# Two octets' stores cut into 112 partitions and 5, 5, 5 and 1, in a linear attention kernel that waits for its DMA engines

## The chip, the cores and the metric

The kernel runs on one core of one Trainium2 chip. The metric is the device time of an execution in microseconds; medians of several executions are quoted. "Span" is the time from the first to the last instruction in a profile; it is about 1.9 us less than the device time.

## The reference

```python
# Q, K, V: [8, 12, 512, 64] float32
Q_feat = np.maximum(0, Q)
K_feat = np.maximum(0, K)
KV = np.einsum('bhkd,bhkv->bhdv', K_feat, V)
K_sum = np.sum(K_feat, axis=2)
numerator = np.einsum('bhqd,bhdv->bhqv', Q_feat, KV)
denominator = np.einsum('bhqd,bhd->bhq', Q_feat, K_sum)
return numerator / (denominator[:, :, :, None] + 1e-10)
```

## The kernel before

The 96 heads are worked on in twelve groups of eight, the octets (`NO` = 12). K, V and Q come in through GpSimd DMAs that cast to bf16. An octet's output, 1 MB of float32 in 128 partitions of 8 KB, is stored by one DMA that SyncE issues and the core's 16 DMA engines carry out; the last octet's store is cut in two along the row. A copy of 128 bytes into `scratch` holds each of the first stores back until the loads five octets ahead have landed.

```python
def store(o, o_sb):
    if o + DELAY < NO:
        nc.sync.dma_start(out=scratch, in_=k_sb[2 * (o + DELAY)][0:1, 0, :])
    parts = 2 if o == NO - 1 else 1
    n = RQ // parts
    for j in range(parts):
        rs = slice(n * j, n * (j + 1))
        nc.sync.dma_start(out=Or[o].rearrange("p (r d) -> p r d", d=D)[:, rs], in_=o_sb[:, rs])
# ... (all else is untouched)
```

## Time and profile before

| | before |
|---|---|
| device time | 127.98 us (median of 3, 127.97 to 128.13) |
| span of the profile | 126.2 us |
| last compute instruction ends | 120.0 us |
| last completion mark of the last store | 125.28 us |
| last instruction | 126.19 us |

How to read it: between 120.0 and 125.28 us nothing but stores runs. The lines of the profile that show the DMA engines' load stand in the prediction below.

Two kinds of records are used besides the profile's views. A *completion mark* is the count of one that each DMA engine adds to a transfer's semaphore (the counter that a waiting engine watches) behind its share of the transfer. It is a packet of 4 bytes. A *packet* is one run of bytes that an engine moves, with its duration. Neither names its engine.

### The profile page before, as it was taken

How to read it: one execution, taken by the hardware profiler on the slowest of the kernel's cores; microseconds unless marked ns; L12 is line 12 of the kernel's file. 1: busy time of each engine (PE TensorE's matmuls, PEld its weight loads, DVE VectorE, ACT ScalarE, POOL GpSimd, SP SyncE). 2: the span in 40 equal slices, each digit the busy share in tenths (PEclk: the TensorE clock that was granted, in tenths of full speed). 3: DMA queues.
4: the chain of work that ended last, by engine and by line, in shares of the span. 5: the costliest groups of instructions: out<-in, count | busy, mean ns of one | idle time of the engine just before them, and what ended most of it. 6: DMA issues, size and time to landing. Idle time of an engine off the chain costs nothing.

```text
span 126.2 us, 4865 instructions
## 1 busy us (share of the span) xinstructions
PE 77.3 (61%) x2112; PEld 68.3 (54%) x2112; DVE 80.6 (64%) x210; ACT 76.9 (61%) x169; POOL 32.1 (25%) x62
## 2 busy tenths in 40 slices
PE   0032917978397956534997647389964793797200
PEld 0041907967386845434986646178953692696100
DVE  3256785698936959673669787528828628774900
ACT  0165891599198798660799949508917925958000
POOL 6902424325243331241143133033113000000000
PEclk9999999999859999996799999955999679769995
DMA  3999999999999999999999999999999999999992
GB/s 106 374 309 213 214 208 209 217 206 218 205 215 209 208 214 324 257 216 325 256 215 301 280 214 281 301 212 214 347 235 216 316 266 216 352 418 410 416 384 104
DMA packets 10757, 32.81 MB, mean 260 GB/s; under 512 B 1392, under 2 KB 1392, under 8 KB 9328
## 3 DMA queue, kind: packets, MB, share of 16 engines
q0 software_dynamic: 8064, 17.83, 73.9%
q1 hardware_dynamic: 2384, 13.63, 27.1%
q10 hardware_dynamic: 288, 1.05, 2.1%
q8 instruction: 16, 0.26, 0.7%
q14 instruction: 5, 0.04, 0.1%
HBM read 37.75 MB, written 12.58 MB: 399 GB/s over the span
## 4 chain that ended last, share of the span: by engine, by line
DMA 32%; PE 27%; issue 13%; ACT 11%; DVE 10%; ACTq 1%; SPq 0%
DMA v_sb<-in_V_dram 25%; PE ps_out L174 13%; PE ps_kv L139 11%; DMA kv_first<-in_K_dram 7%; ACT kvd L146 5%; ACT qt L159 4%; PE ps_qt L153 3%; DVE o_sb L187 3%; DVE qt L121 3%; ACT vo L134 3%; DVE kf L128 2%; DVE vo L130 1%; DVE rec L186 1%; ACTq L267 0%; DVE kvd L118 0%
## 5 line engine op out<-in xcount | busy, mean ns | idle before, releaser
L139 PE MATMUL ps_kv<-vo,kf 128*128 128x130 bf16 x384 | 32.5, 248 | 21.9 <-ACT vo L134 11.7
L174 PE MATMUL ps_out<-kvd,qt 128*32 128x130 bf16 x1536 | 33.7, 243 | 16.7 <-issue 13.3
L139 PEld LDWEIGHTS <-kf 128*128 128x128 bf16 x384 | 27.8, 112 | 25.3 <-DVE vo L130 16.3
L174 PEld LDWEIGHTS <-qt 128*32 128x32 bf16 x1536 | 27.0, 107 | 21.9 <-issue 15.3
L146 ACT CAST kvd<-ps_kv 64x130 bf16<-64x130 f32 x96 | 25.2, 263 | 16.7 <-PE ps_kv L139 14.8
L134 ACT ACTIVATE vo<-v_sb,mask 128x1024 bf16<-128x1024 bf16 x22 | 26.2, 1190 | 13.9 <-DMA v_sb<-in_V_dram 13.8
L187 DVE TENSOR_TENSOR o_sb<-ps_out,rec 128x768 f32<-128x768 f32 (+1 forms) x36 | 31.3, 868 | 1.4
L159 ACT ACTIVATE qt<-ps_qt 128x512 bf16<-128x512 bf16 x48 | 24.8, 603 | 0.3
L128 DVE TENSOR_SCALAR kf<-k_sb,mask 128x1024 bf16<-128x1024 bf16 x44 | 19.1, 476 | 8.6 <-DMA k_sb<-in_K_dram 8.6
L85 POOL DMA_DIRECT2D k_sb<-in_K_dram x22 | 12.8, 583 | 39.1 <-DMA q_sb<-in_Q_dram 24.1
L184 DVE TENSOR_SCALAR den<-ps_out 128x12 f32<-128x12 f32 (+1 forms) x36 | 5.9, 164 | 17.9 <-PE ps_out L174 17.8
L153 PE MATMUL ps_qt<-ident,q_sb 128*128 128x128 bf16 x192 | 15.7, 245 | 2.4 <-issue 2.4
L87 POOL DMA_DIRECT2D v_sb<-in_V_dram x22 | 12.3, 557 | 17.1 <-DMA k_sb<-in_K_dram 7.3
L153 PEld LDWEIGHTS <-q_sb 128*128 128x128 bf16 x192 | 14.0, 112 | 2.6 <-issue 2.5
L130 DVE TENSOR_SCALAR vo<-v_sb,mask 128x1024 bf16<-128x1024 bf16 x22 | 10.6, 481 | 2.1 <-DMA v_sb<-in_V_dram 2.1
L186 DVE RECIPROCAL rec<-den 128x12 f32<-128x12 f32 (+1 forms) x36 | 7.9, 220 | 1.2
L91 POOL DMA_DIRECT2D q_sb<-in_Q_dram x12 | 6.5, 542 | 7.8 <-DMA v_sb<-in_V_dram 4.1
L128 DVE TENSOR_SCALAR kf<-kv_first,mask 128x1024 bf16<-128x1024 f32 x4 | 2.8, 750 | 4.9 <-DMA kv_first<-in_K_dram 4.9
L134 ACT ACT_TABLE_LOAD x1 | 1.3, 1283 | 5.8 <-DMA kv_first<-in_V_dram 5.8
L121 DVE MEMSET qt<- 128x2048 f32 x2 | 3.5, 1765 | 0.8 <-issue 0.8
L134 ACT ACTIVATE vo<-kv_first,mask 128x1024 bf16<-128x1024 f32 x2 | 2.4, 1180 | 2.6 <-DMA kv_first<-in_V_dram 2.6
L130 DVE TENSOR_SCALAR vo<-kv_first,mask 128x1024 bf16<-128x1024 f32 x2 | 1.5, 747 | 0.0
(12 smaller groups left out, 3.5 us busy)
## 6 DMA issues: line engine op xcount, KB each, us to landing
out_dram<-o_sb SPq DMA_DIRECT2D x11, 1024.0 KB, 9.2
q_sb<-in_Q_dram POOLq DMA_DIRECT2D x12, 512.0 KB, 14.9
k_sb<-in_K_dram POOLq DMA_DIRECT2D x22, 256.0 KB, 13.8
v_sb<-in_V_dram POOLq DMA_DIRECT2D x22, 256.0 KB, 13.2
kv_first<-in_V_dram ACTq DMA_DIRECT2D x2, 512.0 KB, 7.3
kv_first<-in_K_dram SPq DMA_DIRECT2D x2, 512.0 KB, 7.0
out_dram<-o_sb SPq DMA_DIRECT2D x2, 512.0 KB, 5.1
scratch<-k_sb SPq DMA_DIRECT2D x7, 0.1 KB, 5.1
```

The lines of the kernel that those rows point to most:

```text
L85: nc.gpsimd.dma_start(out=k_sb[g].rearrange("p r d -> p (r d)"), in_=Kr[g])
L87: nc.gpsimd.dma_start(out=v_sb[g].rearrange("p r d -> p (r d)"), in_=Vr[g])
L128: nc.vector.tensor_scalar(kf[g][:, :, s, :], k_sb[g], scalar1=0.0, scalar2=mask[:, 0, s:s + 1], op0=Alu.max, op1=Alu.mult)
L130: nc.vector.tensor_scalar(vo[g % NB][:, :, 0, 0:D], v_sb[g], scalar1=mask[:, 1, 0:1], scalar2=None, op0=Alu.mult)
L134: nc.scalar.activation(vo[g % NB][:, :, 1, 0:D], v_sb[g], Act.Copy, scale=mask[:, 1, 1:2])
L139: nc.tensor.matmul(ps_kv[g], kf[g][:, r, :, :].rearrange("p s d -> p (s d)"), vo[g % NB][:, r, :, :], start=(r == 0), stop=(r == R - 1), s ...
L146: nc.scalar.copy(kvd[g % NK][64 * c:64 * c + 64, :, s, c, :], ps_kv[g][64 * s:64 * s + 64])
L153: nc.tensor.transpose(ps_qt[o, i][:, u, :], q_sb[o][:, i * (U // 2) + u, :], ident)
L159: nc.scalar.activation(qtz[o % NZ][:, z, us, :, z, :], pv[:, :, :, z, :], Act.Relu)
L174: nc.tensor.matmul(po[hs, b, c:c + 2 * D1], qtf[o % NZ][:, z, u * P + 32 * w:u * P + 32 * w + 32], kvd[(2 * o + h // 4) % NK][:, h % 4 // ...
L186: nc.vector.reciprocal(rec, den)
L187: nc.vector.tensor_tensor(o_sb[:, 2 * u0:2 * (u0 + nu)].rearrange("p (b r) d -> p b r d", b=2), pv[:, :, :, 0:D], rec.unsqueeze(3).to_broa ...
```

## The change

The intent: some DMA engines work off their queues two microseconds before others. Two stores, those of octets 1 and 3, are cut so that engines 0 to 4 take packets from the other eleven: the piece of 112 partitions is meant to leave each engine one packet short of its eight, and the three pieces of 5 are meant for engines 0 to 4 alone. One partition, the *lone row*, is left over. The prediction says by which rule packets go to engines.

```diff
+    def cuts(o):
+        return ((16, P), (0, 5), (5, 10), (10, 15), (15, 16)) if o in (1, 3) else ((0, P),)
...
-        parts = 2 if o == NO - 1 else 1
...
+        Ov = Or[o].rearrange("p (r d) -> p r d", d=D)
+        if o == NO - 1:
+            for j in range(2):
+                rs = slice(RQ // 2 * j, RQ // 2 * (j + 1))
+                nc.sync.dma_start(out=Ov[:, rs], in_=o_sb[:, rs])
+            return
+        for p0, p1 in cuts(o):
+            nc.sync.dma_start(out=Ov[p0:p1], in_=o_sb[p0:p1])
```

More of the change, by code (lines that the diff above doesn't have):

```diff
@@ L197, in store @@
             nc.sync.dma_start(out=scratch, in_=k_sb[2 * (o + DELAY)][0:1, 0, :])
-        parts = 2 if o == NO - 1 else 1
-        n = RQ // parts
-        for j in range(parts):
-            rs = slice(n * j, n * (j + 1))
-            nc.sync.dma_start(out=Or[o].rearrange("p (r d) -> p r d", d=D)[:, rs], in_=o_sb[:, rs])
+        Ov = Or[o].rearrange("p (r d) -> p r d", d=D)
[6 more added lines that the diff above has]
+            nc.sync.dma_start(out=Ov[p0:p1], in_=o_sb[p0:p1])
     zero(0)
```

## The prediction

> **What bounds the kernel now.** I read the page's slices first, then the windows, then the waits and issues of SyncE, then the trace's completion marks of single transfers. Three whole lines of the page's slices and queues:
>
> ```profile
> DMA  3999999999999999999999999999999999999992
> ...
> q0 software_dynamic: 8064, 17.83, 73.9%
> q1 hardware_dynamic: 2384, 13.63, 27.1%
> ```
>
> The mean busy share of the 16 DMA engines is 90% or more in every slice but the first and the last. q0 carries the casting loads; q1 carries the eleven 1 MB stores, the two halves of the last one, and two of the first loads. No compute engine comes near that (the busiest, DVE, is at 64% of the span). The windows view, by stretch (columns: busy us of each engine with its instruction count, clock, DMA share, GB/s):
>
> ```profile
> 75.00:104.00 29.00, 21.04 (x549) 18.49 (x552) 17.09 (x41) 18.09 (x42) 5.66 (x11) 0.82 1.08 264
> 104.00:120.00 16.00, 9.80 (x336) 8.37 (x322) 12.02 (x30) 9.38 (x22) 0.00 (x0) 0.89 1.04 362
> 120.00:121.50 1.50, 0.00 (x0) 0.00 (x0) 0.02 (x1) 0.00 (x0) 0.00 (x0) 1.00 1.00 415
> 121.50:122.50 1.00, 0.00 (x0) 0.00 (x0) 0.00 (x0) 0.00 (x0) 0.00 (x0) 1.00 0.93 381
> 122.50:123.50 1.00, 0.00 (x0) 0.00 (x0) 0.00 (x0) 0.00 (x0) 0.00 (x0) 0.63 0.65 266
> 123.50:124.90 1.40, 0.00 (x0) 0.00 (x0) 0.00 (x0) 0.00 (x0) 0.00 (x0) 0.50 0.38 155
> ```
>
> The reader is to see that a share over 1.00 is possible (packets of one engine overlap a little), that all engines are full up to 121.5 us, and that they then drop out one after another: 0.93, 0.65, 0.38. Compute is over at 120.0. So the kernel ends when the latest DMA engine has worked off its queue, and the idle time of the others between 121.5 and 124.9 is 0.07 + 0.35 + 0.62 x 1.4 = 1.3 us per engine. A perfect balance could win about that and no more.
>
> Who is late can be told from the 16 completion marks that each transfer leaves in the trace, one for each DMA engine. For the last half store (issued at 120.05) they come, counted from the first at 122.76 us, at 0, 0.02, 0.04, 0.07, 0.17, 0.64, 0.77, 1.21, 1.80, 2.16, 2.19, 2.21, 2.23, 2.32, 2.34 and 2.51 us. Five engines are early, eight are over 2.1 us behind the first. The spread is not there at the start (0.6 us for loads landing near 20 us); it is 1.5 at 30 us, 2.7 at 85 us, and the engines keep it. Its growth goes with the 16 instruction fetches:
>
> ```profile
> q8 instruction: 16, 0.26, 0.7%
> ```
>
> Each is one packet of 16 KB that takes 0.88 to 0.97 us on one engine; after the eighth, at 68.1, eight marks of a load stand over a microsecond behind, and after the ninth one mark stands at 2.6 us, so the same eight engines seem to be hit twice. The marks do not name their engine. That the early five are engines 0 to 4 I take from the change's words; the trace as packed can't confirm it.
>
> **What the Trainium skill says.** (1) "Runtime: NRT & Kernel Launch", section Instruction fetch mechanics: instructions are refilled in blocks of 16 KiB by the sequencer's own DMA queue. The trace agrees: 16 packets of 16,384 B on a queue of their own. (2) "DMA: Bandwidth & Descriptors", section Why a DMA increments its semaphore by 16 and not by 1: a transfer issued from SP runs on the largest k up to 16 that divides the slowest dimension, and on the lowest-numbered k engines. So 112 partitions give 7 packets to each of 16 engines, 5 partitions one packet to each of engines 0 to 4. One partition may be split: the 128-byte copies into `scratch` left 112 packets of 8 B in the trace, which is 7 copies over 16 engines, so a lone row of 8 KB would become 16 packets of 512 B. (3) Same page, section The descriptor swizzle: in a 128-partition transfer each engine serves one SBUF port by itself. (4) "SBUF — State Buffer", section Door 1: The DMA port swizzle: partitions 0 to 3 (with 32 to 35) share a port, the next four the next, and one port gives about 27 GB/s. An 8,192 B store packet here takes 309 ns, 26.5 GB/s: one engine alone fills a port. No run here shows two engines on one port.
>
> **The change part by part.** It touches octets 1 and 3 only. Their stores are issued in the middle:
>
> ```profile
> 53.49 0.58 SPq L202 DMA_DIRECT2D out_dram<-o_sb  x1
> ...
> 73.54 0.53 SPq L202 DMA_DIRECT2D out_dram<-o_sb  x1
> ...
> 84.08 0.50 SPq L197 DMA_DIRECT2D scratch<-k_sb  x1
> ```
>
> *Issuing.* Four more DMAs per octet at 0.53 us are 2.1 us of SyncE, in a queue that next acts at 62.9 and at 84.1. Hidden. The eight added DMAs go once round the eight semaphores that these DMAs use in turn, so the stores at the end meet the same ones as before. Seven output buffers take turns, so octet 1's is written again only for octet 8, long after. No new wait.
>
> *Late engines (5 to 15).* Each loses one packet of 8 KB an octet. Packets took 309 to 322 ns, but the durations add up to 1.08 or 1.09 of the time in the middle stretches, so one is worth 0.32 / 1.09 = 0.29 us. The lone row gives back perhaps 0.03 us (estimate: 512 of 8,192 B are 0.02 us, and some for the packet and its mark, 9 ns). Net -0.26 us an octet, **-0.5 us** for two. Being full to the end, these engines end that much earlier: the last mark at 124.75 instead of 125.28.
>
> *Early engines (0 to 4).* By count, +3 - 1 = 2 packets, 0.6 us an octet, 1.2 us for two. They would end at 1.2 to 1.4 us of the scale above, where the late ones end at 2.0. There is room, so by count the sum is -0.5 us: 127.98 - 0.5 = 127.5 us.
>
> *Ports.* By the skill's port table the cost is not only the count. In (0, 5) four engines read partitions 0 to 3 through one port: up to 4 x 0.31 = 1.24 us instead of 0.31. (5, 10) and (10, 15) put two or three on one port: up to 0.93 us each. If the early five run in step, which marks only 0.17 us apart suggest, the three rounds cost up to 3.1 us instead of 0.93, less the 0.31 removed: +2.8 us an octet at worst, 5.6 for two, against 2.5 us of slack. Queue q0's packets between them pull the engines apart and let a port be shared by fewer; I estimate 1 to 2 us an octet. The 112 partitions also no longer start at a port's edge: with seven consecutive ones to an engine, two engines sometimes share a port, and a quarter more time for 7 packets (0.5 us) would eat the gain of the late ones.
>
> **The rivals.** (a) *Count alone*: -0.5 us, 127.5. For it: the engines are full throughout and the lag is carried to the end; the choice of just two octets and five engines fits the marks. Against: it takes the port for free. (b) *Ports cost something*: the late engines gain nothing or lose 0.2 us an octet, the early five use up their slack: 128.0 to 129.2. For it: 26.5 GB/s a packet is a port's rate. Against: reads of SBUF come only from stores, at most half of the packets even during a store, and the queues may overlap behind a stalled packet. (c) *Full contention*: engines 0 to 4 become the new tail, +3 us, 131; it needs all five in step in both octets. (d) *The fetches move*: the eight new DMAs and their waits shift instruction blocks onto other engines, or the early five are not 0 to 4. In the latter case engines with 2.5 us of lag get 1.2 us more: 129.2. SyncE ran only 53 instructions, so that no new block is due. (e) *Hidden anyway*: loads that land 0.5 us sooner change nothing if compute sets the end. Compute ended at 120.0 with over 4 us of stores still queued, so this is unlikely.
>
> **Range and chances.** I give (a) about half, (b) four tenths, (c) and (d) the rest. The middle of that lies at 127.7. Low end: the full 0.6 us of two packets and some luck, 127.2. High end: the upper part of (b), 129.0. Faster by over 2% would need 125.4 us, 2.5 us less, twice what perfect balance gives: 0.01. Slower by over 2% means over 130.5 us, (c) alone: 0.05. Within 2%: 0.94.
>
> **What would show it right or wrong.** Right: the last store's marks span about 1.9 us instead of 2.5, early five at 1.2 to 1.4; the DMA share in the last 3.4 us is higher, its fall later and steeper; the 8 KB packets still take 309 to 322 ns; the queue's 8 KB packets fall from 1,408 to 1,376, with 32 of 512 B if the lone row is split. Ports: some dozens of 8 KB packets with 600 to 1,250 ns, right after 55 and 75 us, and 112-partition packets over 350 ns. A new tail: five marks of the late stores come last. The prediction is wrong if the marks' spread stays at 2.5 us or grows, or if the gain exceeds 1.3 us, which would mean that more than the balance of the end was changed.

## The result, and the profile after

The changed kernel took **127.87 us** (median of 6, 127.73 to 128.08), the kernel before in the same rounds 128.02 us (median of 6, 127.97 to 128.18). The ratio is 0.9987, with a 95% interval of 0.9974 to 1.0. Ratios here are the mean time of one kernel's runs over that of the other's of the same rounds, so not quite the ratio of the medians. Executions over 1.5% slower than the fastest of the same kernel are left out of the means. The gain is about 0.15 us, a quarter to a third of what the count of packets promised; as the interval reaches 1.0, it is not clear of noise.

The page of the changed kernel, the same lines as in the prediction:

```profile
DMA  3999999999999999999999999999999999999992
...
q0 software_dynamic: 8064, 17.83, 74.0%
q1 hardware_dynamic: 2416, 13.63, 27.0%
...
q8 instruction: 16, 0.26, 0.7%
```

The load of the engines is what it was. q1 has 32 packets more, and the trace shows that these are completion marks alone: 384 of 4 bytes instead of 352, while the packets of 8 KB are still 1,408. So the lone row of each cut store was *not* split into pieces of 512 B; it is one packet of 8 KB more on one engine, and leaves one mark: 2 x (16 + 5 + 5 + 5 + 1 - 16) = 32.

SyncE's issues, from the timeline (start, us, instruction, count):

```profile
53.24 1.95 SPq L210 DMA_DIRECT2D out_dram<-o_sb  x5
62.38 0.50 SPq L202 DMA_DIRECT2D scratch<-k_sb  x1
...
73.14 1.87 SPq L210 DMA_DIRECT2D out_dram<-o_sb  x5
83.28 0.50 SPq L202 DMA_DIRECT2D scratch<-k_sb  x1
```

Five DMAs are issued in 1.95 and 1.87 us, and SyncE is next needed over 7 us later: hidden, as predicted. The windows view of the end, with the columns of the prediction (the last two are DMA share and GB/s):

```profile
120.00:121.50 1.50, 0.00 (x0) 0.00 (x0) 0.17 (x1) 0.00 (x0) 0.00 (x0) 0.84 0.98 410
121.50:122.50 1.00, 0.00 (x0) 0.00 (x0) 0.00 (x0) 0.00 (x0) 0.00 (x0) 0.50 1.01 414
122.50:123.50 1.00, 0.00 (x0) 0.00 (x0) 0.00 (x0) 0.00 (x0) 0.00 (x0) 0.50 0.84 344
123.50:124.90 1.40, 0.00 (x0) 0.00 (x0) 0.00 (x0) 0.00 (x0) 0.00 (x0) 0.50 0.22 91
```

Against 0.93, 0.65 and 0.38 of before the share holds longer and then falls more steeply: 1.01, 0.84, 0.22. The balance is better, and yet the end moved little. The 16 completion marks of the last half store show it (us from the span's start):

```
before  122.76 122.78 122.80 122.83 122.93 123.40 123.53 123.97 124.56 124.92 124.95 124.97 124.99 125.08 125.10 125.28
after   122.96 122.98 123.09 123.85 124.06 124.09 124.10 124.12 124.18 124.19 124.28 124.33 124.54 124.58 124.60 125.12
```

Fifteen engines are done by 124.60, 0.68 us before the old end. One is done at 125.12. It alone sets the end, 0.16 us earlier than before. These are single profiles, and the last mark varies: in three further runs that leave every engine its packets (4, 5 and 6 below) it came at 125.42, 125.54 and 125.22 us. So the one mark that stands apart is the finding, not the 0.16 us. Which engine it is, and why, is what the experiments had to find.

### The profile page after: what moved, and what is told of

It is laid out like the page before. It is cut to its first block, busy times and chain, and to the rows that moved or that the text cites. A ratio compares the mean times of both kernels' runs of the same rounds, so it can differ in the third digit from the quotient of the medians.

```text
span 126.0 us, 4878 instructions
## 1 busy us (share of the span) xinstructions
PE 77.5 (62%) x2112; PEld 68.7 (54%) x2112; DVE 80.8 (64%) x210; ACT 77.1 (61%) x169; POOL 31.2 (25%) x62
## 4 chain that ended last, share of the span: by engine, by line
DMA 35%; PE 27%; DVE 13%; issue 13%; ACT 6%; ACTq 1%; SPq 0%; DVEq 0%
DMA v_sb<-in_V_dram 28%; PE ps_out L174 13%; PE ps_kv L139 11%; DMA kv_first<-in_K_dram 7%; DVE o_sb L187 4%; DVE kf L128 3%; PE ps_qt L153 3%; DVE qt L121 3%; ACT kvd L146 3%; DVE vo L130 2%; ACT vo L134 2%; ACT qt L159 2%; DVE rec L186 1%; ACTq L275 1%; DVE den L184 0%
## 5 line engine op out<-in xcount | busy, mean ns | idle before, releaser
L174 PE MATMUL ps_out<-kvd,qt 128*32 128x130 bf16 x1536 | 35.2, 251 | 16.8 <-issue 13.8
L139 PE MATMUL ps_kv<-vo,kf 128*128 128x130 bf16 x384 | 31.5, 242 | 22.9 <-ACT vo L134 12.8
L139 PEld LDWEIGHTS <-kf 128*128 128x128 bf16 x384 | 26.8, 109 | 26.1 <-DVE vo L130 16.7
L174 PEld LDWEIGHTS <-qt 128*32 128x32 bf16 x1536 | 28.6, 111 | 22.0 <-issue 15.5
L85 POOL DMA_DIRECT2D k_sb<-in_K_dram x22 | 12.3, 561 | 39.2 <-DMA q_sb<-in_Q_dram 24.7
L153 PE MATMUL ps_qt<-ident,q_sb 128*128 128x128 bf16 x192 | 15.2, 241 | 1.3 <-issue 1.0
```

The lines of the kernel that those rows point to most:

```text
L85: nc.gpsimd.dma_start(out=k_sb[g].rearrange("p r d -> p (r d)"), in_=Kr[g])
L139: nc.tensor.matmul(ps_kv[g], kf[g][:, r, :, :].rearrange("p s d -> p (s d)"), vo[g % NB][:, r, :, :], start=(r == 0), stop=(r == R - 1), s ...
L153: nc.tensor.transpose(ps_qt[o, i][:, u, :], q_sb[o][:, i * (U // 2) + u, :], ident)
L174: nc.tensor.matmul(po[hs, b, c:c + 2 * D1], qtf[o % NZ][:, z, u * P + 32 * w:u * P + 32 * w + 32], kvd[(2 * o + h // 4) % NK][:, h % 4 // ...
```

## The experiments

**The first suspicion.** The lone row is a packet that engine 0 might carry, which would give it six packets more over the two octets where engines 1 to 4 get four. Theory A said that engine 0 had become the last engine. Theory B said that what the late engines save is lost elsewhere: at the SBUF ports, or by the added DMAs.

**1. The lone row joined to the last piece.**

```diff
-(16, P), (0, 5), (5, 10), (10, 15), (15, 16)
+(16, P), (0, 5), (5, 10), (10, 16)
```

> Octets 1 and 3 as 112 + 5 + 5 + 6 partitions: the same as the change, but the lone row goes to engine 5 and not to engine 0. Theory A (engine 0, with six packets more, has become the last engine): nothing is left on it alone, the last mark comes with the other late engines, 0.5 us earlier than in the changed kernel: span 125.4 to 125.6, time 127.4 to 127.5, one outlier mark less in the last store. Theory B (what the late engines save is lost to ports, extra DMAs or elsewhere): as the changed kernel, 127.8 to 127.9.

Measured: 127.95 us (ratio 0.9998, interval 0.9985 to 1.001). Engine 0 has now no more than engines 1 to 4, and still one mark of the last store stands apart, 125.12 against 124.74. Theory A in this form falls.

**2. One octet only.** The changed kernel's cuts, here for `o in (1,)` alone.

> Only octet 1 cut as 112 + 5 + 5 + 5 + 1. Theory A: engine 0 has three packets more (0.9 us) and is not last; the others lose one packet, 0.3 us: 127.7, better than the changed kernel with two cut octets. Theory B: half of the changed kernel's gain, 127.9 to 128.0.

Measured: 128.00 us (ratio 0.9996, interval 0.998 to 1.0012). The last mark came at 125.11, nothing stands apart (the next is 124.95), and yet the time was not better. By time alone this favours theory B; run 4 shows what may have hidden a gain.

**3. Four octets.** The changed kernel's cuts for `o in (1, 3, 5, 7)`.

> Octets 1, 3, 5 and 7 cut as 112 + 5 + 5 + 5 + 1. Theory A: engine 0 has twelve packets more, 3.6 us on a base near zero, and ends 1.1 to 1.3 us after the tail of before: 129.1 to 129.3, with one mark of the last store standing far behind the others. Theory B: the same small gain again, 127.6 to 127.8.

Measured: 129.13 us (ratio 1.0086, interval 1.0073 to 1.01), as theory A's number had it, but by luck: its sign, one mark far behind the others, did not come. In the last store five marks stand far behind: 125.36, 125.83, 125.91, 126.36 and 126.46, against 124.76 and earlier for the eleven others. These are taken to be the five engines that were added to. Had they started level, four would stand together and one, with the four lone rows, 1.2 us behind them (an estimate: four packets of 0.29 us); they are spread over 1.1 us with no such gap. That was the hint that the five do not start level. The loss is not the tail alone: the last half store was issued at 121.49 us instead of 120.05, and from 120 to 121.5 us the DMA share was 0.72 instead of 1.00. Compute, too, was later here.

**4. A control: cut stores, same balance.** Every engine keeps eight packets, seven and one.

```diff
-(16, P), (0, 5), (5, 10), (10, 15), (15, 16)
+(16, P), (0, 16)
```

> Octets 1 and 3 as 112 + 16 partitions: cut stores, but seven packets and one packet for each of the 16 engines, so no engine's count changes. Both theories of balance: 128.0, as before. If cutting a store or starting it at partition 16 itself saves or costs time, this run shows it.

Measured: 128.47 us (ratio 1.0038, interval 1.0024 to 1.0052). Both theories missed it. The last mark, 125.42, is only 0.14 us later than before; the rest came after it. At its exit SyncE waits for the semaphores of all DMAs, in a fixed order. From the trace, when each of these waits is recorded as done:

```
            semaphore:  107     109     111     112     115     116     117     118
before (last store: 118)  120.55  120.61  120.67  120.73  120.79  122.86  124.08  125.29
control (last store: 109) 124.21  125.44  125.50  125.56  125.62  125.68  125.74  125.80
```

SyncE's and ScalarE's DMAs take eight semaphores in turn. With two DMAs more the last store sits on semaphore 109, and six waits that are long fulfilled still follow its mark, 60 ns each: 0.36 us. In the kernel before and in the changed one (eight DMAs more) the last store sits on 118, the last of the row. Run 1 added six DMAs and has two waits after the mark, run 2 added four and has four. Less 0.12 and 0.24 us they would be at 127.83 and 127.76 us. That arithmetic is mine; runs 5 and 6 test the mechanism.

**5. One added DMA of 2 KB in the kernel before.**

```diff
+    extra = consts.tile([16, D], bf16, name="extra")
...
+        if o == 2:
+            nc.sync.dma_start(out=extra, in_=ident[0:16, 0:D])
```

> The kernel before with one single added DMA of 2 KB, early in the kernel (16 partitions of 128 B). It shifts the semaphores by one, so that the last store's semaphore is the first of its group of eight to be waited for at the exit. Theory of the last waits: seven waits of 60 ns follow the last mark, 0.42 us more: 128.4. Otherwise: 128.0, since 2 KB are nothing.

Measured: 128.37 us against 127.91 (ratio 1.0039, interval 1.0025 to 1.0052): seven waits after the mark, as foretold. What SyncE waited for at its exit, first before, then in this run (total, times, longest, in us):

```profile
SPq L267 <- DMA out_dram<-o_sb: 4.4, 3, 2.0
```

```profile
SPq L270 <- DMA out_dram<-o_sb: 4.6, 1, 4.6
```

Three waits, each for the store that lands next, have become one long wait for the very last one, after which the others are gone through one by one.

**6. A control with eight added DMAs.** Octets 1 and 3 are each stored in five pieces of 16, 16, 16, 16 and 64 partitions, which leave every engine its eight packets ("neutral pieces" below).

> Octets 1 and 3 cut into five neutral pieces each (16, 16, 16, 16 and 64 partitions): every engine keeps its eight packets an octet, and the eight added DMAs bring the last store back to the semaphore that is waited for last. If the 0.48 us of the first control came from six waits of 60 ns after the last store's mark: 128.0 to 128.15, with the last store's semaphore waited for last. If cutting the stores itself costs: 128.5 or more, as four times as many cuts are made.

Measured: 127.92 us against 127.91 (ratio 1.0001, interval 0.9989 to 1.0013). Cutting these two stores costs nothing that can be seen as long as the order of the last waits stays. With this, times can be compared again.

**7. The ports.** The stores of octets 1 to 8 as two DMAs of 64 partitions, eight DMAs more.

> The stores of octets 1 to 8 as two DMAs of 64 partitions each: each engine still carries eight packets of 8 KB an octet, eight DMAs are added, but each DMA reads 64 partitions, half of the ports by the skill's port table, with all 16 engines. Ports theory: packets of 8 KB over 600 ns in the store windows and 1 to 2 us more a store where stores run alone: 130 and more. If ports don't count here: packets stay at 309 to 322 ns and the time at 128.0 to 128.2.

Measured: 129.90 us (median of five runs, 129.0 to 130.76; ratio 1.0155, interval 1.0117 to 1.0194; one slow run of 132.09 is left out). The answer is split in time, and the packets of 8 KB tell it. In the stretches up to 104 us, where loads run between stores, their median is 322 ns and five of 768 took over 400 ns, exactly as many as before. After 104 us, where stores follow stores and the loads come to an end (the last lands at 111.8 us), 88 of 640 took over 400 ns (7 before), up to 1,166, and their mean is 354 ns (313 before). The windows view of this run from 104 us to 120 us and at the end:

```profile
104.00:120.00 16.00, 9.26 (x347) 7.80 (x344) 12.06 (x30) 9.38 (x22) 0.00 (x0) 0.99 1.04 319
...
123.50:124.90 1.40, 0.00 (x0) 0.00 (x0) 0.00 (x0) 0.00 (x0) 0.00 (x0) 0.50 0.93 377
124.90:126.50 1.60, 0.00 (x0) 0.00 (x0) 0.00 (x0) 0.00 (x0) 0.00 (x0) 0.50 0.30 120
```

The engines are as busy as before (1.04) but move 319 GB/s instead of 362. So stores cut into halves go with slower packets, but only where stores follow stores. Of the 88 slow packets 45 took 500 to 650 ns, about twice the usual 309, which fits two engines at one port; no run cuts stores in that stretch without sharing ports, so the cause of this slowdown is argued, not shown. (Run 3, whose fourth cut store falls into the stretch, has 17 packets over 400 ns there.) Octets 1 and 3 store in the stretch where loads run between: in the changed kernel the longest of the 8 KB packets that start between 53 and 63 us took 322 ns, and of those between 73 and 84 us all but two took at most 322 (one 689, as one did before with 664, and one 333). Theory B's ports are out for this change.

**8. Who is late: probes.** Eight tiny DMAs of 1, 2, 3, 4, 5, 6, 8 and 12 partitions were queued right behind the store of octet 10; a DMA of k partitions is taken to leave marks of engines 0 to k - 1, by the rule on k that the prediction quotes (the probe of a single row was split over all 16). Each probe of 2 and more partitions has one record more than k; the first one, which comes by itself 1.0 to 1.7 us after the probe is issued (at 119.42 us for the probe of 4 before the change), is left out. What the probe of k + 1 shows beyond that of k is engine k; each further probe on an engine adds 0.17 us. The kernels give right results; their times (130.23, 130.56 and 130.44 us) miss the expected 128.0 by over 2 us and are of no use: the last half store, issued at 120.05 us without probes, was issued at 124.05 us or later with them.

```diff
+    KS = (1, 2, 3, 4, 5, 6, 8, 12)
+    probe = [consts.tile([k, D], bf16, name=f"probe{k}") for k in KS]
...
+            if o == NO - 1:
+                for k, t in zip(KS, probe):
+                    nc.sync.dma_start(out=t, in_=ident[0:k, 0:D])
```

> The kernel before with eight tiny probes (64 bf16 a partition, 1, 2, 3, 4, 5, 6, 8 and 12 partitions) queued right behind the store of octet 10; a probe of k partitions runs on k engines, so its k completion marks tell how late those engines are. If engines 0 to 4 are the early ones, the marks of the probe of 5 all lie within 0.3 us of the first mark of octet 10's store, and the probe of 12 shows marks more than 2 us later. If they are not, the marks of the probe of 5 lie elsewhere in the spread. Time within 0.3 us of 128.0; eight extra DMAs leave the order of the last waits as it is.

> The changed kernel with the same probes. Theory A (the lone row has made engine 0 the last one): the single mark of the probe of 1 is the latest of all, 0.4 us or more behind the rest, and the marks of engines 1 to 4 come well before it. Theory C (engine 0 is level with 1 to 4, and the latest engine is one of the eleven others, hit by the last instruction fetch): the marks of the probe of 5 end earlier than the last mark of octet 10's store.

> The variant 112 + 5 + 5 + 6 with the same probes. Here engines 0 to 4 have four packets more each and the latest mark of the last store was still 0.4 us behind the others. Theory A': the latest is one of engines 0 to 4 (the probe of 5 has the latest mark). Theory C: the latest is outside, the probe of 5 ends before it.

Measured, from the marks: when each engine had worked off octet 10's store. An example, the kernel before: the probe of 4 has marks at 120.56, 120.64, 121.30 and 121.71. Three of them are the marks of the probe of 3 (120.38, 120.47 and 121.54) plus 0.17; so 121.30 is new and is engine 3. One step of 0.18 back is the mark 121.12 of the first probe, which ran on all 16 engines, and one more step back the store's own mark at 120.94. Engine 4 is the new mark of the probe of 5 (us):

```
before   probe of 4  120.56 120.64 121.30 121.71
         probe of 5  120.73 120.82 121.48 121.88 122.22
changed  probe of 4  122.30 122.53 122.57 122.76
         probe of 5  122.47 122.71 122.75 122.93 123.37
```

Two steps back from 122.22 are the first probe's 122.04 and the store's 121.85; two steps back from 123.37 are 123.19 and 123.00.

| us | engines 0 and 1 (in order of time) | 2 | 3 | 4 | 5 | latest of all |
|---|---|---|---|---|---|---|
| before | 119.85 and 121.02 | 120.12 | 120.94 | 121.85 | 122.64 | 122.65 |
| changed | 121.85 and 122.07 | 121.78 | 122.17 | **123.00** | 122.09 | **123.00** |
| 112 + 5 + 5 + 6 | 121.15 and 122.08 | 121.36 | 121.97 | **122.73** | 122.52 | **122.73** |

Each row is one profile. Theory A of these expectations (engine 0 is last) and theory C (the last engine is one of the other eleven) both fail; A' (it is one of engines 0 to 4) holds. Before the change engines 0 to 4 are *not* the early five: they stand 0 and 1.2 (engines 0 and 1; which is which follows below), 0.3, 1.1 and 2.0 us behind the first mark. Engine 4 with its 2.0 us gets 1.15 us more and becomes the last, in the changed kernel and in run 1. (Engine 3 gets 1.23 and engine 2 1.66 us more; in run 1's cut it is 1.03 and 1.24, and 0.88 for engine 4.) Engine 5, with two packets less, gains 0.55 us; in run 1's cut, which gives it the two packets back, it stands 0.12 us from where it was. Engine 0 with its lone rows is not the last. The table also tells engines 0 and 1 apart: in run 1's cut both get four packets more, and against it the changed kernel gives engine 0 two more still, about 0.6 us. That fits if engine 0 is the early one (121.15 to 121.85, engine 1 at 122.08 and 122.07), and not the other way round (122.08 to 121.85 or less). So engine 0 stood at 0 us and engine 1 at 1.2. In the changed kernel the three earliest marks of the store, 119.41, 119.46 and 119.91 us, belong to none of engines 0 to 5: the change took packets from early engines too.

**9. Engine 4 spared.** Octet 1 is stored in 112 + 4 + 4 + 4 + 4 partitions, octet 3 in the neutral pieces of run 6, to keep the order of the last waits.

```diff
+        if o == 1:
+            return ((16, P), (0, 4), (4, 8), (8, 12), (12, 16))
+        return ((0, 16), (16, 32), (32, 48), (48, 64), (64, P)) if o == 3 else ((0, P),)
```

> Octet 1 as 112 + 4 + 4 + 4 + 4, so that engines 0 to 3 carry three packets more and the twelve others, engine 4 among them, one less; octet 3 in five neutral pieces, so that the order of the last waits stays. Theory A' (engine 4 is the one that the change makes last): no outlier, all late engines 0.3 us earlier, 127.6 to 127.75. If instead engines 1 or 3 become last, or the gain is lost elsewhere: 127.85 to 128.0.

Measured: 127.67 us against 127.91 (ratio 0.9984, interval 0.9969 to 0.9999). No mark stands apart: 124.59, 124.79, 124.85 and 124.99 are the last. One cut octet that spares engine 4 gains about as much as two that don't (ratio 0.9984 against 0.9987), and the last mark is 0.29 us earlier than before, the worth of one packet.

**10. The same cut twice.** Octets 1 and 3 both as 112 + 4 + 4 + 4 + 4.

> Octets 1 and 3 both as 112 + 4 + 4 + 4 + 4: engines 0 to 3 carry six packets more each (1.8 us), the twelve others two less (0.55 us); the order of the last waits stays. By the probes of the kernel before, engines 0 to 3 stand 0, 1.2, 0.3 and 1.1 us behind its first mark and the latest engine 2.8. Theory A': engines 1 and 3 become last at 3.0, the time is 127.9 to 128.2, no better than before, and two marks stand apart at the end. If engines 0 to 3 were all early: the late ones set the end, 127.4 to 127.5.

Measured: 128.11 us against 128.01 (ratio 1.0007, interval 0.9994 to 1.0021). Two marks stand apart, at 125.29 and 125.30; the fourteen others end at 124.51. They are taken to be the two that the probes put at 1.2 and 1.1 us (marks name no engine), and the time is that of before; both were foretold.

Run 9 is the best version found. Its interval ends just below 1, and against the changed kernel (0.9987) it was not timed in the same rounds, so it is shown to beat the kernel before, barely, and not shown to beat the changed one.

## Why the prediction was right or wrong

The time lay in the range and within 2%, near the stated middle: 127.87 against 127.7. That nearness is luck: it lies between what rival (a) gave, 127.5, and what rival (b) gave, 128.0 and more, and neither's account is what happened. By its steps:

- *What bounds the kernel*: right. The end is the latest DMA engine's: runs 9 and 10 put the last mark at 124.99 and 125.30 us, close to where the count of packets, added to the probes' lags, puts it (an estimate: 0.29 us earlier than before for run 9, 0.1 us later for run 10).
- *Issuing hidden, no new wait*: right. The remark that eight added DMAs leave the semaphores' order as it was turned out to be worth 0.1 to 0.4 us: runs 1, 2, 4 and 5 lost that much for want of it.
- *Late engines, -0.5 us for two packets*: right, as far as single profiles tell. Engine 5 gained 0.55 us by the probes; all but one engine were done 0.68 us before the old end.
- *Early engines, "There is room"*: this is the step that failed. It rests on "That the early five are engines 0 to 4 I take from the change's words". The probes show 0 to 2.0 us. The size of the addition was roughly right (1.2 us forecast; 1.15 on engine 4, 1.23 and 1.66 on engines 3 and 2), the base was not. So engine 4 went from 2.0 to beyond the others, and ended within 0.16 us of the old end. Rival (d) named this case, but for all five engines at once, with a loss; it held for one.
- *The lone row perhaps split*: wrong. It is one packet of 8 KB; it added to an engine that could bear it. The count of 1,376 packets was a slip besides: two rows split would have left 1,406 of the 1,408.
- *Ports, rival (b)*: the time that (b) gave, 128.0 to 129.2, did not come, and its cause was absent where the change stores. Run 7 shows packets slowed elsewhere, where it may be the cause.
- *Full contention (c)*: no packet in the store windows of octets 1 and 3 came near its 1.24 us (the longest took 0.69).
- *The fetches move*, the other half of (d): the changed kernel has 16 fetches as before, each within 1.0 us of its old time; on which engines they fell no record tells.
- *The signs*: that the spread of the last marks would shrink to 1.9 us was off (2.16, with 1.64 but for the last mark), and engines 0 to 4 stood at 2.4 to 3.6 us in the probe run, not at 1.2 to 1.4; the unchanged packets of 8 KB and the steeper fall of the DMA share came as described.

What stays open: why engine 4 is late. By the marks the instruction fetches seem to put back eight engines, and it may be one of them, but no record names the engine of a fetch, and no run changes the fetches.

## What to carry to other kernels

When DMA engines are the bound, find out which engine is late before moving packets: in this kernel a DMA of few rows behind a long one left marks of a few engines alone, and the differences of such probes told them apart. Shift from the latest to those with room, and stop when an added-to engine catches up. And when a change adds or removes a DMA, compare the waits at the program's exit: here 0.1 to 0.4 us of them hid what run 2 may have gained and made the neutral run 4 slower.

## What the Trainium skill lacked or had wrong

- "Runtime: NRT & Kernel Launch", section Instruction fetch mechanics, calls the cost of crossing a 16 KiB block mostly hidden, and does not say which DMA engines carry the fetches. Here each of the 16 fetches holds a DMA engine for 0.88 to 0.97 us, and these engines are the bound; after the first one a mark stood 0.9 us behind the next-latest (1.54 against 0.61 us). What the fetches cost in device time no run shows.
- "SBUF — State Buffer", section Door 1: The DMA port swizzle, gives rates by the ports that a transfer reaches. It lacks what a narrow store costs among casting loads: here nothing that can be seen, as its 8 KB packets stayed at 322 ns. Cut stores had slow packets only where stores ran back to back (run 7: 88 of 640 over 400 ns; that ports are the cause there is not shown).
- "DMA: Bandwidth & Descriptors", section Why a DMA increments its semaphore by 16 and not by 1, lacks when a single row is split over the engines: here the rows of 128 bytes were (112 packets of 8 bytes for seven copies), the lone rows of 8 KB, written with three dimensions in the kernel, were not.
- No page has the cost of the exit: SyncE's waits for the eight semaphores of SyncE's and ScalarE's DMAs, in a fixed order, 60 ns each even when fulfilled; one added DMA of 2 KB made the kernel 0.4 to 0.5 us slower.
